# Value projections of a dilated attention: activation columns taken in token order, the head groups' orders made when the values are read back

## The chip, the cores and the metric

The kernel runs on one core of a Trainium2 chip. The metric is the device time of one execution in microseconds; the kernel before has a median of 1347.46 us over three runs (1345.95 to 1347.58). Engines are named as the profile names them: PE is TensorE (PEld its weight loads), DVE is VectorE, ACT is ScalarE, POOL is GpSimd, SP is SyncE, which here issues nearly all DMAs. A matmul on PE has two operands from on-chip memory (SBUF): a stationary one of 128 x 128, which a weight load puts into the array, and a moving one, which is streamed past it.

## The reference

One decoder block on x of 1024 tokens x 1024 features, batch 1. After a norm with a scale and shift from a conditioning vector, one projection `h @ w_in` gives q, k, v, a gate z, beta and a decay for eight heads of a gated delta rule (branch A), q, k, v and z for twelve heads of 64 features of a dilated sliding-window attention (branch B), and two merge gates. The two branches are projected, gated, added, projected once more and added to x; a final norm ends it. What matters here is branch B:

```python
DIL_CONFIGS = ((128, 1), (512, 4), (2048, 16))   # (window, dilation) of the head groups 0, 1, 2
...
qb, kb, vb, zb = ...                             # columns of h @ w_in
for gi, (win, dil) in enumerate(DIL_CONFIGS):    # four heads each
    o_g, lse_g = dilated_window_attention(qb[:, :, hs], kb[:, :, hs], vb[:, :, hs], win, dil)
```

Query t attends the keys t - j * dilation. So the tokens of a group fall into classes of equal remainder, and the kernel works through a group's tokens class by class: group 0 in token order, group 1 in four classes (t mod 4) of 256 tokens, group 2 in eight classes (t mod 8) of 128 tokens, where a mask does the rest of the dilation of 16.

## The kernel before, in words

Everything is fp32. A projection with full precision is made of three products: activations and weights are each split into a high part (fp32r) and a low remainder, and hi x hi, hi x lo and lo x hi are accumulated. The transposed activations hT (features on the 128 partitions, 1024 tokens along the free axis) lie in SBUF as eight pairs (hi, lo) of 128 x 1024 tiles, one pair for each block kk of 128 features.

Most projections are feature-major: the weights are stationary, hT is moving, and a tile of 128 features x 1024 tokens takes 48 matmuls of 128 x 512. The value projections of the attention, which the program calls B0, B1 and B2 for the head groups 0, 1, 2, are token-major: hT is stationary (`cols(hi)` and `cols(lo)`), the split weights (tiles named wh) are moving, 256 columns wide (272 for B0, which has beta and the decay in it). Each has eight tiles of 128 tokens, taken in pairs i2 = 0..3; a pair goes through the eight feature blocks with two tiles x three products each, so that a stage has 4 x 8 x 6 = 192 matmuls. In the profile they are the rows `pj<-wh,big`, where big is hT.

The stationary operand of such a matmul is 128 columns of hT. `v_cols` says which: for B0 128 neighbouring tokens, for B1 every fourth token, for B2 every eighth. So the PSUM tiles come out in the group's order. ACT copies each pair into one of two tiles big of 128 x 1024 (four token tiles of 256 values side by side), and at the stage's end SP writes both to a DRAM buffer vbd of 128 x 2048, as they lie. Much later `attn_group` reads them back, as they lie, when it has room for them, and the attention's last products take 64 columns of them as stationary operands.

All streams of work (one for each head, each weight unit, each attention worker) are generators; a scheduler at build time (`Sched`) books each instruction on an estimated clock and picks by priority, so the order on each engine is fixed in the program. At run time each engine takes its instructions in that order and waits at semaphores. The projections are the stream of lowest priority and fill PE. Between their matmuls stand the small products of the delta rule's recurrence (`rec_stream`: rows `sb<-sq,TT`, `sb<-sq,big`), where each step needs a result of DVE or ACT. The program order of the projections is in four parts, one for each pair of heads (`ORDER`): B0 is the third tile of the first part and B1 its last, B2 is the last of the second part.

Weights come by DMA into one of two tiles wr, are split by ACT (hi) and DVE (lo) into a pair of the six tiles wh, and are freed after their last matmul. A value projection holds three weight units, all six tiles wh, through its four pairs; they become free in the last pair, after kk = 2, 5 and 7.

Times in the profile have one line for nearly all instructions, line 96 (the helper `Engine.call`), so that tiles and shapes tell them apart.

Of the kernel before, what the change touches and what calls it, by code (L numbers as in the profile page):

```python
# [7 lines left out]
F32 = mybir.dt.float32  # L8
# [5 lines left out]
DRAM = bass.MemoryType.DRAM  # L14

P = 128
T = 1024
# [33 lines left out]
class Slots:  # L51
    """Live-tile accounting for one tag, so that a tile is asked for only when one is free."""

# [6 lines left out]
    def get(self, dtype=F32, shape=None, add=None, owed=0):  # L60
        """add: a tile that promises so many later ones; owed: one (1) of those."""
        while len(self.free_at) <= (0 if add is None else self.debt + add):
            yield lambda: len(self.free_at) > (0 if add is None else self.debt + add)
        self.debt += (add or 0) - owed
        self.free_at.sort()
        t = self.free_at.pop(0)
        if t > self.s.now():
            yield t
        self.count += 1
        return self.pool.tile(shape or self.shape, dtype, tag=self.tag, name=f"{self.tag}{self.count}")  # L70
# [15 lines left out]
class Engine:  # L86
    """An engine of the core whose issued work is also booked on an estimated clock."""

# [14 lines left out]
class Sched:  # L103
    """Orders the instructions: every stream is a generator that yields where it waits."""

# [69 lines left out]
    def chain(self, e, n=1):  # L175
        """n operations on engine e each need the result of the one before."""
        self.clk[e] += 125 * n
        self.cur.done[e] += 125 * n
        self.cur.last = max(self.cur.last, self.cur.done[e])
# [73 lines left out]
def hybrid_block_kernel(ctx: ExitStack, tc: tile.TileContext, x, c, norm_w, ada_w, ada_b, w_tiles, w_vb0, w_vb1,  # L253
# [26 lines left out]

    # ---- constants and small parameters
    cst = const([P, 1056], "cst")
# [26 lines left out]
    xd_d = [dp.tile([64, T], F32, name=f"xd{i}") for i in range(4)]  # L309
    vb_d = [dp.tile([P, 2048], F32, name=f"vbd{g}") for g in range(3)]  # L310
    ya_d = [dp.tile([P, T], F32, name=f"yad{h}") for h in range(H)]
# [22 lines left out]

    # ---- start: x, statistics, transposes
    def load_start():
# [62 lines left out]
    def consts_start():  # L399
        dve.memset(pw[:, 0], -0.5)  # L400
        dve.memset(pw[:, 1], 0.5)
        for i in range(2):
            pool.memset(TT[i], 0.0)
            pool.memset(Xb[i], 0.0)
        dve.memset(one_row, 1.0)
        yield ev_row
        # silu(c) on every partition
        for hf in range(2):
            pb = yield from sb.get()
            pe.matmul(pb, one_row, scb[1][0:1, hf * 512:(hf + 1) * 512], start=True, stop=True)  # L410
            yield
            if hf == 0:
                scb[0] = yield from big.get()
            act.activation(scb[0][:, hf * 512:(hf + 1) * 512], pb, AF.Silu)
            sb.put()
        big.put()
        S.set(ev_mod)
# [90 lines left out]

    # ---- weights: load, split into two exact parts
    class W:  # L510
# [44 lines left out]

    # ---- products with both operands split
    def three(pt, whi, wlo, khi, klo, first, last):
# [5 lines left out]

    # ---- the kinds of output tiles
    KT, QT, VT, ZT = {}, {}, {}, {}
# [71 lines left out]

    # ---- projection program
    prog = []
# [61 lines left out]

    def v_cols(g, i):
        """Token positions of tile i in the order of group g, as columns of the transposed activations."""
        if g == 0:
            return lambda t: t[:, i * P:(i + 1) * P]
        if g == 1:
            r, ub = divmod(i, 2)
            return lambda t: t.rearrange("p (u r) -> p r u", r=4)[:, r, ub * P:(ub + 1) * P]
        return lambda t: t.rearrange("p (u r) -> p r u", r=8)[:, i, :]

    def v_evac(pt, g, i2, last):
        vt = VB[g]
        n = 272 if g == 0 else 256
        src = pt.rearrange("p (a b) -> p a b", a=2)
        dst = vt[i2 // 2].rearrange("p (a b) -> p a b", a=4)
        a0 = (i2 % 2) * 2
        act.activation(dst[:, a0:a0 + 2, :], src[:, :, 0:256], AF.Copy)
        if g == 0:
            dve.tensor_copy(ba[:, 2 * i2:2 * i2 + 2, :], src[:, :, 256:272])
        pj.put()  # L720
        if last:
            if g == 0:
                S.set(ev_ba)
            yield
            for q in range(2):
                sp.dma_start(vb_d[g][:, q * T:(q + 1) * T], vt[q])
            big.put(2)
            S.set(ev_vbd[g])
# [3 lines left out]
    def projections():  # L732
        # the first tiles go contraction-outermost, behind the preparation of h
        pts = []
        for q in range(FIRST):
            kind, idx, u = prog[q]
# [37 lines left out]
        for n, (kind, idx, u) in enumerate(prog):  # L774
# [3 lines left out]
            if kind == "vB":  # L778
                w = 272 if idx == 0 else 256
                VB[idx] = []  # L780
                for _ in range(2):
                    t = yield from big.get(add=0)
                    VB[idx].append(t)
                for i2 in range(4):
                    pt = yield from pj.get()
                    for kk in range(8):
                        uu = u[kk // 3]
                        if i2 == 0:
                            yield uu.ev
                        c0 = (kk % 3) * w  # L790
                        hi, lo = hT[kk]
                        for i in (2 * i2, 2 * i2 + 1):
                            cols = v_cols(idx, i)
                            o = pt[:, (i % 2) * 512:(i % 2) * 512 + w]
                            pe.matmul(o, cols(hi), uu.hi[:, c0:c0 + w], start=kk == 0, stop=False)
                            pe.matmul(o, cols(hi), uu.lo[:, c0:c0 + w], start=False, stop=False)
                            pe.matmul(o, cols(lo), uu.hi[:, c0:c0 + w], start=False, stop=kk == 7)
                        if i2 == 3 and kk in (2, 5, 7):
                            wh.put(2)
                        yield S.now()  # L800
                    S.add(v_evac(pt, idx, i2, i2 == 3), 10, f"vB{idx}{i2}")
                continue
# [10 lines left out]
            S.add(finish(kind, idx, pt), 10, f"{kind}{idx}")  # L813
        # merge phase
        yield from tail_products()

    # ---- gates of the delta rule, for all heads
    def stats_stream():
# [41 lines left out]

    # ---- delta rule, one head
    DT, KP, NT, AT, VR = {}, {}, {}, {}, {}
# [21 lines left out]
    def d_stream(h):  # L884
        """exp of the sum of g over the tokens after the row's, up to the column's."""
        yield [ev_g, ev_stats]
# [70 lines left out]
    def inv_stream(p):  # L957
# [5 lines left out]
        yield  # L963
        # the inverse grows in the lower triangles, the factors stay in the upper ones
        pool.memset(xv[:, 0:T:33], 1.0)
# [103 lines left out]
    def qsum_stream(h):  # L1069
        """Squares of q summed over its features, tokens on the partitions."""  # L1070
        yield ev_q[h]
# [18 lines left out]
    def turn(src, dst, bounce):  # L1090
        """Transposes every 128 x 128 block: 32 x 32 blocks on VectorE, which then change places through DRAM.

        Columns of dst: (quarter of a block's rows, block, row in the quarter)."""
        t = yield from big.get()
# [20 lines left out]
    def rec_stream(h):  # L1115
# [55 lines left out]
        big.put(5)  # L1171
        # norm over the head, gate, feature-major
        q8, m8 = qss[:, h], mo[:, h]
# [19 lines left out]

    # ---- dilated attention
    OG = {}
# [3 lines left out]
    def attn_unit(g, i2, ti):  # L1199
        """Two tiles of 128 queries, feature tile ti (two heads, in the two halves of the rows)."""  # L1200
        qt, kt = QB[2 * g + ti], KB[2 * g + ti]
# [62 lines left out]
        if pend[g] == 8:  # L1264
            S.set(ev_og[g])

    def attn_group(g):
        yield [ev_vbd[g], ev_qb[2 * g]]
        VB[g] = []
        for q in range(2):  # L1270
            t = yield from big.get(owed=1)
            sp.dma_start(t, vb_d[g][:, q * T:(q + 1) * T])
            VB[g].append(t)
# [108 lines left out]

    # ---- merge and output
    YA, YB, MG, WO, M = {}, {}, {}, {}, {}
# [87 lines left out]
    def rows_stream():  # L1472
        """gate and the final norm's weights, along the free axis on every partition."""
        yield ev_mg[0]
# [53 lines left out]
    def tail_products():  # L1528
# [15 lines left out]

        # two tiles side by side while their operand is still being prepared
        for j, kk in [(j, k_ - 2 * j) for k_ in range(10) for j in range(2) if 0 <= k_ - 2 * j < 8]:
# [109 lines left out]
def _layout(inp):  # L1656
    """The arrays as the program takes them: moved around, never computed on."""
    import numpy as np
# [60 lines left out]
```

## Time and profile before

| | |
|---|---|
| median of three runs | 1347.46 us |
| span of the profiled execution, first to last instruction | 1343.9 us |
| own total of the profiled execution | not recorded apart; the median is 3.6 us above the span |
| PE busy | 1307.5 us, 97% of the span |
| PEld busy | 1095.1 us, 81% |
| DVE, ACT, POOL busy | 690.3, 494.3, 146.4 us |
| granted PE clock, mean | 0.995 |
| DMA | 137.65 MB, 102 GB/s on average |
| stage B0 | 76.4 to 100.9 us |
| stage B1 | 231.0 to 289.1 us, the recurrence of heads 0 and 1 beside it |
| stage B2 | 440.2 to 491.7 us, the end of the recurrence of heads 2 and 3 beside its first part |
| values read back | from 839.2, 872.8 and 941.7 us |

[...] A row of the timeline is a run of like instructions: start in us, length in us, engine, line, operation, tiles, count. Rows with DMA_DIRECT2D on SPq are the issues of DMAs, not the transfers.

### The profile page before, as it was taken

Reading aid. Unit: us, or ns where it says so; the run is one execution under the profiler, and the core shown is the slowest. Engines: PE = TensorE matmul, PEld = TensorE weight load, DVE = VectorE, ACT = ScalarE, POOL = GpSimd, SP = SyncE. Lnnn points to the kernel's source line nnn. Section 1 sums busy time; section 2 is a strip of 40 time slices with the busy share of each in tenths; the row PEclk is TensorE's granted clock in tenths of the full one; section 3 lists DMA queues with packets and bytes.
Section 4 is the critical chain, followed back from the end, with each engine's and each line's share of the span. In section 5 each row is a group of like instructions: output and inputs, shape, how many; then the busy total and the mean of one; then the engine's idle time right before and its main releaser. Section 6 shows DMA issues by size and latency. Waiting matters only on the chain.

```text
span 1343.9 us, 18856 instructions
## 1 busy us (share of the span) xinstructions
PE 1307.5 (97%) x7386; PEld 1095.1 (81%) x7386; DVE 690.3 (51%) x1437; ACT 494.3 (37%) x1054; POOL 146.4 (11%) x97
## 2 busy tenths in 40 slices
PE   5899899999999999999999999999999999999997
PEld 3698688998888998888888888877777888888886
DVE  6767762147873137873478734232323136745533
ACT  5637213246233226233462334253536432212211
POOL 4502100023000112000230002000000000001500
PEclk9899999999999999999999999999999999999999
DMA  9336421043321152322243212411111165342422
GB/s 361 105 120 180 103 87 47 25 136 120 105 77 35 32 188 67 106 72 71 86 138 106 78 49 94 144 62 33 64 38 35 41 222 159 119 141 107 152 99 94
DMA packets 72266, 137.65 MB, mean 102 GB/s; under 512 B 30161, under 2 KB 38769, under 8 KB 72178
## 3 DMA queue, kind: packets, MB, share of 16 engines
q1 hardware_dynamic: 72034, 136.20, 32.0%
q8 instruction: 58, 0.95, 0.3%
q14 instruction: 30, 0.25, 0.1%
q10 hardware_dynamic: 144, 0.26, 0.1%
HBM read 105.84 MB, written 30.59 MB: 102 GB/s over the span
## 4 chain that ended last, share of the span: by engine, by line
PE 90%; DMA 4%; DVE 4%; issue 1%; ACT 0%; SPq 0%; POOL 0%; POOLq 0%; DVEq 0%; ACTq 0%
PE pj L96 76%; PE sb L96 14%; DVE big L96 3%; DMA wr<-in_w_tiles_dram 1%; DMA vtd<-big 1%; DMA big<-in_ada_w_dram 1%; DVE wh L96 1%; DMA big<-in_x_dram 0%; DMA big<-grow 0%; SPq L96 0%; DVE mod L96 0%; DMA big<-vtd 0%; ACT wh L96 0%; ACT big L96 0%; POOL big L96 0%
## 5 line engine op out<-in xcount | busy, mean ns | idle before, releaser
L96 PE MATMUL pj<-big,wh 128*128 128x512 f32 x3840 | 941.9, 398 | 11.1 <-POOL big L96 6.3
L96 PEld LDWEIGHTS pj<-big,wh 128*128 128x128 f32 x3840 | 706.3, 189 | 157.4 <-POOL big L96 7.8
L96 ACT ACTIVATE wh<-wr 128x1024 fp32r<-128x1024 f32 (+3 forms) x96 | 95.6, 996 | 322.0 <-PE pj L96 301.6
L96 DVE TENSOR_TENSOR wh<-wr,wh 128x1024 fp32r<-128x1024 f32 (+3 forms) x93 | 114.8, 1236 | 158.2 <-ACT wh L96 158.0
L96 PE MATMUL pj<-wh,big 128*128 128x256 f32 (+2 forms) x702 | 155.7, 373 | 0.0
L96 PEld LDWEIGHTS pj<-wh,big 128*128 128x128 f32 x702 | 142.2, 267 | 5.3 <-POOL wh L96 0.4
L96 ACT ACTIVATE big<-big 128x1024 f32<-128x1024 f32 (+1 forms) x61 | 64.5, 1059 | 149.3 <-DVE big L96 117.9
L96 DVE SCALAR_TENSOR_TENSOR big<-pj,cw,big 128x1023 f32<-128x1023 f32 (+2 forms) x66 | 84.4, 1279 | 1.8 <-ACT big L96 0.3
L96 PEld LDWEIGHTS sb<-sq,big 128*128 128x128 f32 x464 | 63.0, 192 | 4.4
L96 PE MATMUL sb<-sq,big 128*128 128x128 f32 x464 | 65.5, 274 | 0.0
L96 DVE TENSOR_TENSOR big<-big,big 128x1024 f32<-128x1024 f32 (+3 forms) x40 | 55.0, 1381 | 15.4 <-ACT big L96 13.3
L96 ACT ACTIVATE big<-pj 128x1024 f32<-128x1024 f32 (+1 forms) x56 | 51.7, 923 | 29.3 <-PE pj L96 29.2
L96 ACT ACTIVATE mid<-sb 128x384 f32<-128x384 f32 (+5 forms) x75 | 34.1, 461 | 66.9 <-PE sb L96 66.5
L96 DVE SCALAR_TENSOR_TENSOR sq<-sq,gsm,sb 128x128 f32<-128x128 f32 x48 | 16.6, 345 | 81.8 <-PE sb L96 80.4
L96 POOL TENSOR_TENSOR wh<-wr,wh 128x1024 fp32r<-128x1024 f32 x3 | 9.0, 3009 | 398.2 <-ACT wh L96 398.1
L96 ACT ACTIVATE mid<-mid,sta 128x128 f32<-128x128 f32 (+1 forms) x96 | 42.2, 441 | 25.5 <-DVE sta L96 25.5
L96 DVE COPY big<-sb 128x256 f32<-128x256 f32 (+1 forms) x32 | 12.4, 389 | 74.0 <-PE sb L96 73.9
L96 PE MATMUL pj<-big,big 128*128 128x512 f32 x210 | 49.1, 389 | 0.0
L96 POOL TENSOR_TENSOR mo<-mo,pw 128x8 f32<-128x8 f32 x8 | 13.1, 1636 | 325.2 <-DVE mo L96 325.2
L96 PE MATMUL sb<-big,big 128*128 128x128 f32 (+4 forms) x365 | 45.5, 316 | 1.8 <-DVE big L96 1.8
L96 ACT ACT_TABLE_LOAD x29 | 37.2, 1283 | 26.2 <-DVE big L96 22.4
L96 PEld LDWEIGHTS pj<-big,big 128*128 128x128 f32 x210 | 39.4, 188 | 8.2
(124 smaller groups left out, 1115.1 us busy)
## 6 DMA issues: line engine op xcount, KB each, us to landing
wr<-in_w_tiles_dram SPq DMA_DIRECT2D x64, 512.0 KB, 3.8
big<-in_ada_w_dram SPq DMA_DIRECT2D x24, 512.0 KB, 9.0
big<-in_x_dram SPq DMA_DIRECT2D x16, 512.0 KB, 4.7
gd<-big SPq DMA_DIRECT2D x16, 512.0 KB, 5.0
big<-gd SPq DMA_DIRECT2D x16, 512.0 KB, 4.7
big<-grow SPq DMA_DIRECT2D x8, 512.0 KB, 5.1
vtd<-big SPq DMA_DIRECT2D x8, 512.0 KB, 3.0
big<-vtd SPq DMA_DIRECT2D x32, 128.0 KB, 3.7
```

The source lines that it names most:

```text
L96: r = f(*a, **k)
```

## The change

The three value projections take 128 neighbouring tokens as the stationary operand, in all groups. The DRAM buffers vbd become 1024 tokens x 256 values: row t holds token t. The write at a stage's end puts each token tile into its rows; the read makes the group's order by its access pattern (`v_load`).

```diff
-    vb_d = [dp.tile([P, 2048], F32, name=f"vbd{g}") for g in range(3)]
+    vb_d = [dp.tile([T, 256], F32, name=f"vbd{g}") for g in range(3)]
...
-    def v_cols(g, i):
-        if g == 0:
-            return lambda t: t[:, i * P:(i + 1) * P]
-        if g == 1:
-            r, ub = divmod(i, 2)
-            return lambda t: t.rearrange("p (u r) -> p r u", r=4)[:, r, ub * P:(ub + 1) * P]
-        return lambda t: t.rearrange("p (u r) -> p r u", r=8)[:, i, :]
...
     def v_evac(pt, g, i2, last):
...
+            rows = vb_d[g].rearrange("(i p) f -> p i f", p=P)
             for q in range(2):
-                sp.dma_start(vb_d[g][:, q * T:(q + 1) * T], vt[q])
+                sp.dma_start(rows[:, 4 * q:4 * q + 4], vt[q].rearrange("p (a f) -> p a f", a=4))
...
     def projections():
...
                         for i in (2 * i2, 2 * i2 + 1):
-                            cols = v_cols(idx, i)
+                            cs = slice(i * P, (i + 1) * P)
                             o = pt[:, (i % 2) * 512:(i % 2) * 512 + w]
-                            pe.matmul(o, cols(hi), uu.hi[:, c0:c0 + w], start=kk == 0, stop=False)
-                            pe.matmul(o, cols(hi), uu.lo[:, c0:c0 + w], start=False, stop=False)
-                            pe.matmul(o, cols(lo), uu.hi[:, c0:c0 + w], start=False, stop=kk == 7)
+                            pe.matmul(o, hi[:, cs], uu.hi[:, c0:c0 + w], start=kk == 0, stop=False)
+                            pe.matmul(o, hi[:, cs], uu.lo[:, c0:c0 + w], start=False, stop=False)
+                            pe.matmul(o, lo[:, cs], uu.hi[:, c0:c0 + w], start=False, stop=kk == 7)
...
+    def v_load(g, q, t):
+        t4 = t.rearrange("p (a f) -> p a f", a=4)
+        if g == 0:
+            sp.dma_start(t4, vb_d[g].rearrange("(i p) f -> p i f", p=P)[:, 4 * q:4 * q + 4])
+        elif g == 1:
+            src = vb_d[g].rearrange("(b p r) f -> r p b f", b=2, r=4)
+            for a in range(2):
+                sp.dma_start(t4[:, 2 * a:2 * a + 2], src[2 * q + a])
+        else:
+            sp.dma_start(t4, vb_d[g].rearrange("(p r) f -> p r f", r=8)[:, 4 * q:4 * q + 4])
...
     def attn_group(g):
...
-            sp.dma_start(t, vb_d[g][:, q * T:(q + 1) * T])
+            v_load(g, q, t)
```

The order of the instructions on PE, DVE, ACT and POOL is the same in both kernels, one for one. Only SP's queue differs. At the end of B1, where the values of group 1 (vbd_119) are written (two tiles big, between the loads of the next weights wr), the two issues stay where they were:

```order
 L96 DMA wr_2429<-in_w_tiles_dram 128x1024
-L96 DMA vbd_119<-big_2001 128x1024
-L96 DMA vbd_119<-big_2002 128x1024
+L96 DMA vbd_119<-big_2001 128x4x256
+L96 DMA vbd_119<-big_2002 128x4x256
 L96 DMA wr_2470<-in_w_tiles_dram 128x1024
```

Each partition's 1024 values now go to four places of 256 values (1 KB) in place of one of 4 KB. At the place where the values of group 1 are read back for the attention, two issues became four, again between the same loads of weights:

```order
 L96 DMA wr_7173<-in_w_tiles_dram 128x1024
-L96 DMA big_7338<-vbd_119 128x1024
-L96 DMA big_7340<-vbd_119 128x1024
-L96 DMA wr_7344<-in_w_tiles_dram 128x1024
-L96 DMA wr_7561<-in_w_tiles_dram 128x1024
+L96 DMA big_7338<-vbd_119 128x2x256 x2
+L96 DMA big_7341<-vbd_119 128x2x256 x2
+L96 DMA wr_7346<-in_w_tiles_dram 128x1024
+L96 DMA wr_7563<-in_w_tiles_dram 128x1024
```

Groups 0 and 2 are read with two issues each as before, group 0 in pieces of 1 KB, group 2 in runs of 4 KB (four rows that are neighbours).

## The prediction

> **What bounds the kernel now.** I read the page first: the engines' busy times and the chain that ended last.
>
> ```profile
> PE 1307.5 (97%) x7386; PEld 1095.1 (81%) x7386; DVE 690.3 (51%) x1437; ACT 494.3 (37%) x1054; POOL 146.4 (11%) x97
> PE 90%; DMA 4%; DVE 4%; issue 1%; ACT 0%; SPq 0%; POOL 0%; POOLq 0%; DVEq 0%; ACTq 0%
> ```
>
> PE is busy nearly throughout and makes 90% of the chain that ended last. What PE saves in a stage is saved in the end, unless another engine was just hidden behind that stage. Next, PE's matmuls grouped by shape, for the value projections (`pj<-wh,big`; the row of 272 columns is B0, that of 256 columns is B1 and B2 together):
>
> ```profile
> L96 PE MATMUL pj<-wh,big 128*128 128x256 f32 x384 | 100.7, 409 | 0.0
> L96 PE MATMUL pj<-wh,big 128*128 128x272 f32 x192 | 24.5, 288 | 0.0
> ```
>
> Twice as many matmuls of fewer columns take four times as long: 100.7 / 384 = 262 ns of busy time each against 24.5 / 192 = 128 ns. The two rows differ in width, and in the step between the stationary columns. So I look at the weight loads, first by stage for these tiles alone (columns: stretch, its length, PE busy, PEld busy, DVE, ACT, POOL, clock, DMA share, GB/s), then by duration in B0, B1 and the last part of B2:
>
> ```profile
> 76.40:100.90 24.50, 24.39 (x194) 24.13 (x193) 1.95 (x2) 2.62 (x3) 0.00 (x0) 1.00 0.39 131
> 230.96:289.11 58.15, 51.31 (x193) 47.18 (x194) 3.13 (x3) 2.74 (x3) 0.00 (x0) 1.00 0.12 38
> 440.16:491.73 51.57, 49.10 (x193) 47.24 (x193) 3.13 (x3) 2.12 (x2) 0.00 (x0) 1.00 0.23 72
> ```
>
> ```profile
> L96 PEld LDWEIGHTS pj<-wh,big 128*128 128x128 f32 x105 | 13.2, 188 | 0.0
> L96 PEld LDWEIGHTS pj<-wh,big 128*128 128x128 f32 x192 | 47.2, 329 | 0.0
> L96 PEld LDWEIGHTS pj<-wh,big 128*128 128x128 f32 x90 | 21.7, 337 | 0.0
> ```
>
> A load of 128 neighbouring columns lasts 188 ns (B0), of every fourth 329 ns (B1), of every eighth 337 ns (B2). The clock is 1.00 in all three stages, so it isn't the clock. In B1 and B2 the loads are back to back (47.2 us for 192, 246 ns each) and the matmuls wait for them. Steps of 4 and of 8 cost the same.
>
> What would 256 columns cost with a dense load? The timeline of the kernel's end has such matmuls, and that of B2's undisturbed part the slow ones:
>
> ```profile
> 470.04 21.85 PE L96 MATMUL pj<-wh,big 128*128 128x256 f32 x90
> 491.73 22.41 PE L96 MATMUL pj<-big,wh 128*128 128x512 f32 x98
> 513.98 0.60 PE L96 MATMUL sb<-cst,big 128*128 128x128 f32 x4
> ```
>
> ```profile
> 1331.59 1.96 PE L96 MATMUL sb<-big,big 128*128 128x256 f32 x15
> 1333.39 1.24 PE L96 MATMUL sb<-wh,big 128*128 128x256 f32 x9
> ```
>
> Start to start, 15 dense ones take 1333.39 - 1331.59 = 1.80 us, 120 ns each; 90 strided ones take 491.73 - 470.04 = 21.69 us, 241 ns each. B0's 272 columns at 24.13 / 192 = 126 ns agree with 120 for 256.
>
> **The change part by part.** *The loads become dense.* B1 and B2 need 47.18 + 47.24 = 94.4 us of PE for 384 pairs of load and matmul; at 120 ns they need 46.1. Gross gain 48.3 us.
>
> *The changes between streams.* A dense run pays something where PE goes over to the recurrence's products, which a strided run partly hides. In the second pair's recurrence, beside dense matmuls of 512 columns:
>
> ```profile
> 417.85 0.70 PE L96 MATMUL pj<-big,wh 128*128 128x512 f32 x2
> 418.39 0.61 PE L96 MATMUL sb<-sq,big 128*128 128x128 f32 x4
> ```
>
> In the long run after B2 one such matmul takes (513.98 - 491.73) / 98 = 227 ns; two between small products take 418.39 - 417.85 = 0.54 us, 0.09 more than 2 x 0.227. B1 has 25 such runs and B2 has 12 (rows of the timeline from 230.96 on, the last of them the one at 470.04), so 37 x 0.09 = 3.3 us come back.
>
> *The recurrence beside it.* A step of heads 0 and 1 in B1, PE's rows and then ACT's (in brackets the idle time ahead and what ended it):
>
> ```profile
> 245.97 0.60 PE L96 MATMUL sb<-sq,TT 128*128 128x128 f32 x4
> 246.33 1.67 PE L96 MATMUL pj<-wh,big 128*128 128x256 f32 x6
> 247.83 1.05 PE L96 MATMUL sb<-sq,big 128*128 128x128 f32 x8
> ```
>
> ```profile
> 246.56 0.59 ACT L96 ACTIVATE big<-pj 128x512 f32<-128x512 f32 x1
> 247.04 0.28 ACT L96 ACTIVATE sq<-sb 128x128 f32<-128x128 f32 x1
> ```
>
> PE goes from the four TT products to the eight that need ACT's two copies `sq<-sb` in 1.86 us: 0.36 for its own four and 1.50 for six strided matmuls. With dense ones it is there after 0.36 + 6 x 0.12 + 0.09 = 1.17 us. The second copy ends 247.32 - 245.97 = 1.35 us after the start, since a copy of the value projection (0.59) stands ahead of it in ACT's queue; so half of the eight wait some 0.2 us, and this happens only where a pair of value tiles is copied out. The other hand-overs lack that copy, which leaves 1.35 - 0.59 = 0.76 us against 1.17. And the row at 417.85 shows a cover of 0.54 us between two dependent groups, where the dense B1 has 0.81. I take 1 us for all waits. The bounds are 0 and 0.3 us at each of the 37 runs, 11.1 us; behind a waiting product stand only the next value matmuls, on PE itself. Nearest to the rows is the low end.
>
> *The next weights.* All six tiles wh are held until the last pair, so the split of the next weights sits in the last 30 matmuls:
>
> ```profile
> 98.36 1.23 DVE L96 TENSOR_TENSOR wh<-wr,wh 128x1024 fp32r<-128x1024 f32 x1 [1.07 <-ACT wh L96]
> ...
> 484.49 1.06 ACT L96 ACTIVATE wh<-wr 128x1024 fp32r<-128x1024 f32 x1 [3.48 <-PE pj L96]
> 485.58 1.23 DVE L96 TENSOR_TENSOR wh<-wr,wh 128x1024 fp32r<-128x1024 f32 x1 [8.51 <-ACT wh L96]
> ```
>
> In B2 the split ends at 486.81 and PE needs it at 491.73: 4.92 us of room, of which 30 x 0.121 = 3.6 go. 1.3 us are left, as many as B0, dense already, has between 98.36 + 1.23 = 99.59 and its end at 100.9, without a stall (24.39 us of its 24.50 are busy with these tiles). B1 has more (the recurrence is between). Behind that wait in ACT's and DVE's queues are only the recurrence's last steps. Cost 0; if the cover were gone, one split, 1.06 + 1.23 = 2.3 us in each stage.
>
> *Where the room goes.* All instructions in B1 and in B2, columns as above:
>
> ```profile
> 230.96:289.11 58.15, 58.15 (x310) 58.15 (x309) 13.46 (x41) 17.30 (x56) 0.97 (x1) 1.00 0.12 38
> 440.16:491.73 51.57, 51.57 (x242) 51.57 (x240) 11.17 (x28) 10.25 (x30) 7.07 (x4) 1.00 0.23 72
> ```
>
> DVE has 13.5 of 58.2 us in B1 and 11.2 of 51.6 in B2, ACT 17.3 and 10.3, so neither carries a backlog out of the stage when it is 22 us shorter. What runs on DMA time across B2's end is the row of g for the next head:
>
> ```profile
> 487.28 0.38 SPq L96 DMA_DIRECT2D big<-grow  x1
> ...
> 494.65 1.68 DVE L96 TENSOR_TENSOR_SCAN big<-big,cst 128x128 f32<-128x128 f32 x5
> ```
>
> It is issued 4.4 us before the stage's end, later 0.9 before it, lands (5.1 us, below) about 4.2 after the end, and its scan on DVE begins 2.9 after now: about 1.3 us late. Behind it in DVE's queue are convolutions and splits of tiles that PE needs from 10 us after the end on. Cost 0; without that cover 1.3 us.
>
> *The DMAs.* The six writes and the reads of groups 0 and 1 go in pieces of 1 KB, and six issues of reads become eight. The DMAs by tile (count, KB each, us from issue to landing), and the first read beside the first products that use it:
>
> ```profile
> big<-grow SPq DMA_DIRECT2D x8, 512.0 KB, 5.1
> ...
> big<-vtd SPq DMA_DIRECT2D x32, 128.0 KB, 3.7
> ...
> vbd<-big SPq DMA_DIRECT2D x6, 512.0 KB, 5.3
> ```
>
> ```profile
> 839.21 1.27 SPq L96 DMA_DIRECT2D big<-vbd  x2
> ...
> 880.79 0.88 PE L96 MATMUL sb<-mid,big 128*64 128x128 f32 x12
> ```
>
> The reads of vtd have pieces of 1 KB: 3.7 us for 128 KB. So a transfer of 512 KB lies between 5.3 us (no change) and 4 x 3.7 = 14.8 (four of these one after the other), nearer the lower, since a fourth of the bytes takes 3.7 as well. The read at 839 has 41 us until its use, so even 2 x 14.8 us is hidden. Each more issue costs SP 1.27 / 2 = 0.6 us, ahead of a weight load that two tiles wr cover. Below nothing the cost can't be, as nothing gets shorter there. Cost 0 to 2 us (a write ahead of the weight loads); I take 0.
>
> *Sum.* 48.3 - 3.3 - 1 = 44.0 us. The span goes from 1343.9 to 1299.9. The median of the runs is 3.6 above that span, so **1303.5 us**.
>
> [...]
>
> **The rivals.** *The waits take over*: the hand-overs of the recurrence set the pace in B1 and B2, each near its bound. Gain 48.3 - 3.3 - 11.1 = 33.9, and with late splits 2 x 2.3 less: 29.3 to 33.9, about 1316 us. For it: PE's cover of each hand-over nearly halves. Against: the 0.54 us of cover at 417.85 without a stall, and B0's end.
>
> *Half the gain*, in one of two ways. Only the step of 8 pays, so that B1 keeps its time: 47.24 - 23.04 - 12 x 0.09 = 23.1 us less, 1324 us; against it B1's 329 ns. Or the 188 ns of a dense load aren't hidden: 384 x (0.246 - 0.188) = 22.3 us less, 1325 us; against it B0. [...]
>
> *The change doesn't do what it says*: the 256-column matmuls are slow for a reason other than the step, and nothing moves, 1347 us. Against it: the 120 ns at the kernel's end.
>
> *Slower*: the pieces of 1 KB block the DMA queues ahead of weight loads, at the three writes and the reads of groups 0 and 1. If they went one after the other at the row of vtd, 1 MB would take 8 x 3.7 = 29.6 us; the cover is the tile that PE is on, 48 x 0.227 = 10.9 us; so PE would stall 18.7 us at each of five places, 93.5 us, and the time would be 1303.5 + 93.5 = 1397 us. It decides the sign from 44 / 5 = 8.8 us at each place on, that is when 1 MB takes 19.7 us or more. Against: it takes about twice 5.3 now, and the DMA engines are 0.12 and 0.23 busy in B1 and B2.
>
> **How the numbers follow.** Forecast 0.85, the waits take over 0.08, half the gain 0.03, nothing moves 0.02, slower 0.02. The range holds the forecast with its unknowns. Low end: no price for the changes between streams and no waits, gain 48.3, and 1 us for the spread of the runs: 1298. High end: the waits' upper bound without late splits, gain 33.9: 1313. A difference over 0.2%, 2.7 us, is about what a measurement of this kernel can tell from no change: faster 0.96 (the first three cases), same 0.02, slower 0.02.
>
> **What would show it.** In the changed profile: LDWEIGHTS of `pj<-wh,big` at about 188 ns in all three stages; the row of 256 columns at about 46 us busy in place of 100.7 (some more, as runs beside small products overlap); B1 about 36 us long, B2 about 28; DVE, ACT and POOL with the same busy times; the stretch from 492 to the end as long as before. Wrong would be it if the loads stay at 330 ns, or if B1 stays above 45 us with PE waiting for DVE or ACT at `sb` rows, or if a later stretch grows by more than 2 us, first of all where `big<-vbd` or `vbd<-big` is followed by a late `wr`.

## The result, and the profile after

The changed kernel takes 1300.57 us in the median of four runs (1299.39 to 1300.83), the kernel before 1347.05 (1345.95 to 1347.58, four runs). The ratio is 0.9654, with a 95% interval of 0.964 to 0.9667: 46.5 us or 3.5% faster. The profiled execution has a span of 1299.0 us and a time of 1300.81.

The page of the changed kernel, engines' busy times and the chain that ended last:

```profile
PE 1261.6 (97%) x7386; PEld 1049.0 (81%) x7386; DVE 690.9 (53%) x1437; ACT 494.3 (38%) x1054; POOL 145.4 (11%) x97
PE 82%; issue 7%; DVE 6%; DMA 3%; POOL 1%; ACT 1%; SPq 0%; POOLq 0%; DVEq 0%; ACTq 0%
```

PE lost 45.9 us of busy time and PEld 46.1; DVE, ACT and POOL kept theirs within 1 us. PE is still busy for 97% of the span and stays the bound. The chain has less of PE in it than before (82% against 90%): at a wait of PE that is shown below it goes over to the other engines, back to POOL at 267 us, and the 71.6 us for which POOL had then been idle are counted as issue. The groups by shape of the changed kernel, B1 and B2 first, then B0, then all weight loads of these tiles (126 for matmuls of 512 columns among them), and those of the kernel before:

```profile
L96 PE MATMUL pj<-wh,big 128*128 128x256 f32 x384 | 54.8, 290 | 0.0
...
L96 PE MATMUL pj<-wh,big 128*128 128x272 f32 x192 | 24.5, 288 | 0.0
...
L96 PEld LDWEIGHTS pj<-wh,big 128*128 128x128 f32 x702 | 95.9, 189 | 5.2 <-DVE big L96 0.2
```

```profile
L96 PEld LDWEIGHTS pj<-wh,big 128*128 128x128 f32 x702 | 142.2, 267 | 5.3 <-POOL wh L96 0.4
```

The row of 256 columns fell from 100.7 to 54.8 us; that of B0, which the change leaves alone on PE, is the same to the tenth. A load's mean fell from 267 to 189 ns. Neighbouring matmuls overlap in these rows: 384 of 290 ns make 111 us, and the group is busy for 54.8; so busy times and distances from start to start are compared here, not mean durations. The stages by windows, first of the changed kernel (ahead of B1 nothing differs; columns: stretch, length, PE, PEld, DVE, ACT, POOL busy, clock, DMA share, GB/s), then of the kernel before:

```profile
231.21:266.84 35.63, 35.63 (x310) 35.63 (x308) 12.97 (x39) 16.83 (x55) 0.00 (x0) 1.00 0.17 50
266.84:418.86 152.02, 151.24 (x957) 126.99 (x955) 103.03 (x215) 60.32 (x130) 20.92 (x12) 1.00 0.34 100
418.86:447.02 28.16, 28.16 (x242) 28.16 (x240) 9.51 (x26) 10.15 (x30) 7.07 (x4) 1.00 0.28 93
447.02:1299.00 851.98, 844.51 (x4697) 691.94 (x4695) 417.01 (x866) 306.04 (x667) 67.21 (x41) 1.00 0.31 99
```

```profile
289.11:440.16 151.05, 151.05 (x955) 127.07 (x955) 102.02 (x212) 60.13 (x129) 19.95 (x12) 1.00 0.33 98
491.73:1343.90 852.17, 844.59 (x4696) 692.00 (x4695) 415.17 (x864) 305.76 (x667) 68.09 (x41) 1.00 0.31 98
```

| stretch | before, us | after, us | difference |
|---|---|---|---|
| start to B1 | 230.96 | 231.21 | +0.25 |
| B1 | 58.15 | 35.63 | -22.52 |
| between B1 and B2 | 151.05 | 152.02 | +0.97 |
| B2 | 51.57 | 28.16 | -23.41 |
| B2 to the end | 852.17 | 851.98 | -0.19 |
| span | 1343.9 | 1299.0 | -44.9 |

All of the gain is in the two stages, and 0.97 us of it is given back between them. Of these, 0.78 us are one wait of PE behind B1; the other 0.19 us are busy time (151.24 us against 151.05) that no row explains. The timeline of PE has the wait:

```profile
270.43 18.42 PE L96 MATMUL pj<-big,wh 128*128 128x512 f32 x80
289.62 0.66 PE L96 MATMUL sb<-cst,big 128*128 128x128 f32 x4 [0.78 <-ACT big L96]
```

PE waits 0.78 us for a result of ACT (in brackets the idle time and what ended it), ahead of the transposes of a new head's k. Before, it went from its 80 matmuls to these transposes without a wait.

### The profile page after: what moved, and what is told of

It is laid out like the page before. It is cut to its first block, busy times and chain, and to the rows that moved or that the text cites. A ratio compares the mean times of both kernels' runs of the same rounds, so it can differ in the third digit from the quotient of the medians.

```text
span 1299.0 us, 18858 instructions
## 1 busy us (share of the span) xinstructions
PE 1261.6 (97%) x7386; PEld 1049.0 (81%) x7386; DVE 690.9 (53%) x1437; ACT 494.3 (38%) x1054; POOL 145.4 (11%) x97
## 4 chain that ended last, share of the span: by engine, by line
PE 82%; issue 7%; DVE 6%; DMA 3%; POOL 1%; ACT 1%; SPq 0%; POOLq 0%; DVEq 0%; ACTq 0%
PE pj L96 69%; PE sb L96 13%; DVE big L96 4%; DMA big<-in_x_dram 1%; DMA vtd<-big 1%; DVE wh L96 1%; POOL big L96 1%; DVE mod L96 1%; DMA big<-grow 0%; ACT big L96 0%; DVE mid L96 0%; DMA big<-otd 0%; SPq L96 0%; POOL mo L96 0%; DMA otd<-big 0%
## 5 line engine op out<-in xcount | busy, mean ns | idle before, releaser
L96 PE MATMUL pj<-wh,big 128*128 128x256 f32 (+2 forms) x702 | 109.5, 307 | 0.0
L96 PEld LDWEIGHTS pj<-wh,big 128*128 128x128 f32 x702 | 95.9, 189 | 5.2 <-DVE big L96 0.2
L96 DVE TENSOR_TENSOR mid<-big 64x31 f32<-64x31 f32 (+15 forms) x124 | 41.1, 332 | 9.0 <-POOL big L96 5.6
```

The lines of the kernel that those rows point to most:

```text
L96: r = f(*a, **k)
```

## The experiments

Each is told against runs of the kernel before on the same chip, beside it (medians 1346.2 to 1346.5 us; a single run beside the two wide kernels).

### Each stage alone

```diff
# b1_dense, against the changed kernel (B2 strided again, B1 dense)
+    def v_cols(g, i):
+        if g < 2:
+            return lambda t: t[:, i * P:(i + 1) * P]
+        return lambda t: t.rearrange("p (u r) -> p r u", r=8)[:, i, :]
...
+                if g == 2:
+                    sp.dma_start(vb_d[g].rearrange("(p r) f -> p r f", r=8)[:, 4 * q:4 * q + 4], v4)
```

> B1 takes neighbouring tokens, B2 still every eighth; the buffers hold token rows and the reads make the order, as in the change. Theory (the cost sits in the loads of stationary columns at a step, on PE alone, and adds up by stage): B1 shrinks by 22.5 us as in the changed kernel, B2 stays at 51.6, and the stall of 1 us after B1 comes with it: 1347.0 - 22.5 + 1.0 = 1325.5 us, between 1324 and 1327. [...] Rival (part of the gain came from the transfers): outside 1324 to 1327, and the two halves don't add up to 46.5.

> B2 takes neighbouring tokens, B1 still every fourth. Theory: B2 shrinks by 23.4 us, nothing after it stalls: 1347.0 - 23.4 = 1323.6 us, between 1322 and 1325. Rival (only the step of 8 paid): 1300.6, the whole gain. Rival (the transfers have a part in it): the gains of the two halves differ from 46.5 us in sum by more than 2.

b2_dense is the mirror image: B1 strided, its values written class by class with four DMAs, B2 dense. Measured: b1_dense 1324.67 us (ratio 0.9836, 0.9822 to 0.9849), b2_dense 1323.02 us (0.9823, 0.9809 to 0.9836), beside 1346.52. The gains are 21.9 and 23.5 us, 45.4 in sum; the whole change gave 46.5. So each stage pays for itself, and a step of 4 costs about as much as a step of 8. The rival of the prediction by which only the step of 8 pays is out.

### The transfers alone, and the loads alone

```diff
# dma_only, against the changed kernel: v_cols as in the kernel before, and in v_evac
+                if g == 1:
+                    src = vb_d[g].rearrange("(b p r) f -> r p b f", b=2, r=4)
+                    for a in range(2):
+                        sp.dma_start(src[2 * q + a], v4[:, 2 * a:2 * a + 2])
+                elif g == 2:
+                    sp.dma_start(vb_d[g].rearrange("(p r) f -> p r f", r=8)[:, 4 * q:4 * q + 4], v4)
# dense_old_dma, against the kernel before
-        if g == 0:
-            return lambda t: t[:, i * P:(i + 1) * P]
...
+        return lambda t: t[:, i * P:(i + 1) * P]
```

> Both stages still take their tokens at a step; the values go to the token rows of the new buffers (group 1 by four writes) and are read back by the new patterns. Theory (the pieces of 1 KB are hidden): 1347.0 within 1 us. Rival (the pieces cost, and the change's gain is net of them): 1349 or more, with a late weight load behind vbd rows.

> The columns are neighbours in all three stages, the buffers and transfers are those of the kernel before. Left out: the order of the values of groups 1 and 2 is not made, so the attention of these groups reads other tokens' values; the work is the same. Theory: the change's time, 1300.6 within 1 us. Rival (the new transfers cost): 1 to 3 us below the change. Rival (they help by shorter transfers): above it.

dma_only: 1346.56 us beside 1346.52, ratio 0.9997 (0.9988 to 1.0006). dense_old_dma: 1301.43 us, 0.9662 (0.9649 to 0.9675), which can't be told from the change's 0.9654. The reads of dma_only are those of the change, its writes are not (group 1 in four writes, group 2 in runs of 4 KB); the change's own writes are tested by dense_old_dma, which lacks them and lies 0.9 us from the change. The transfers neither cost nor gain anything that these runs resolve. The DMAs of the changed kernel by tile (count, KB each, us from issue to landing), and SP's issues where group 1 is read back:

```profile
vbd<-big SPq DMA_DIRECT2D x6, 512.0 KB, 5.4
...
big<-vbd SPq DMA_DIRECT2D x4, 512.0 KB, 5.6
...
big<-vbd SPq DMA_DIRECT2D x4, 256.0 KB, 5.2
```

```profile
828.14 1.97 SPq L96 DMA_DIRECT2D big<-vbd  x4
846.12 25.05 SPq L96 DMA_DIRECT2D wr<-in_w_tiles_dram  x2
```

Pieces of 1 KB land in the time of pieces of 4 KB (5.4 us against 5.3 for the writes), and the four issues end 16 us ahead of SP's next weights.

### Which step costs what

Steps of 2 and of 3 fp32 lie between the dense load (120 ns a pair) and the steps of 4 and 8 (246 ns a load in both stages). My forecasts, 1300 to 1304 us for step2 and 1324 for step3, rest on an assumption about the load that no run shows.

```diff
# step2: B1 and B2 take every second token of a block of 256
+        return lambda t: t.rearrange("p (b u r) -> p b r u", b=4, r=2)[:, i // 2, i % 2, :]
# step3: every third
+        return lambda t: t[:, 80 * i:80 * i + 382:3]
```

> As the change, but B1 and B2 take every second token (two classes in each block of 256 tokens), 8 bytes from column to column; the writes put them into token rows. [...] Rival (any step takes the slow way, 241 ns): 1346.5. Rival (the cost grows evenly with the step, half way between 1 and 4 at 2): around 1315.

> As the change, but B1 and B2 take every third token, 12 bytes apart, from a start of 80 columns times the tile's number. Left out: the values of groups 1 and 2 are those of other tokens; the work is the same. [...] Rival (any step but 1, or any step over 2): 1346.

step2 takes 1302.26 us (0.9668, 0.9652 to 0.9683), step3 1322.49 (one run). B2's run without other products between, of the changed kernel (step 1), of step2 and of step3:

```profile
436.14 11.04 PE L96 MATMUL pj<-wh,big 128*128 128x256 f32 x90
447.02 22.41 PE L96 MATMUL pj<-big,wh 128*128 128x512 f32 x98
```

```profile
437.86 11.05 PE L96 MATMUL pj<-wh,big 128*128 128x256 f32 x90
448.75 21.49 PE L96 MATMUL pj<-big,wh 128*128 128x512 f32 x94
```

```profile
452.40 15.93 PE L96 MATMUL pj<-wh,big 128*128 128x256 f32 x90
468.17 22.42 PE L96 MATMUL pj<-big,wh 128*128 128x512 f32 x98
```

| step of the columns, fp32 | 1 | 2 | 3 | 8 (kernel before) |
|---|---|---|---|---|
| start to start, us for 90 | 10.88 | 10.89 | 15.77 | 21.69 |
| ns a pair of load and matmul | 121 | 121 | 175 | 241 |

A step of 4 costs as much as one of 8 (47.18 and 47.24 us for 192 loads in the kernel before). Up to there the pair's time goes nearly with the step: 175 / 3 = 58 and 241 / 4 = 60 ns for each fp32 of step. By these two numbers I estimate 117 to 121 ns for a load at a step of 2, no more than the dense pair's 121, so that beside 256 columns it would not show; measured, the pair takes 121. The loads' own durations in these runs of 90, of the changed kernel, step2 and step3, go the same way (337 ns at a step of 8):

```profile
L96 PEld LDWEIGHTS pj<-wh,big 128*128 128x128 f32 x90 | 10.9, 192 | 0.0
```

```profile
L96 PEld LDWEIGHTS pj<-wh,big 128*128 128x128 f32 x90 | 10.9, 195 | 0.0
```

```profile
L96 PEld LDWEIGHTS pj<-wh,big 128*128 128x128 f32 x90 | 15.8, 262 | 0.0
```

If any step were slow, step2 would lie at 1346, and if steps below 4 cost nothing, step3 would lie at 1301; both are out: a step of 2 costs nothing beside 256 columns, 3 costs 54 ns a pair, and 4 costs as much as 8. Why the cost grows up to a step of 4 and is the same at 8 was not shown; pairs of neighbours at a far step would say more, and weren't tried.

### Whether the load hides behind a wider matmul

```diff
# wide_dense, against the changed kernel; wide_step, the same against dma_only
-                        c0 = (kk % 3) * w
+                        c0, w = ((kk % 3) * 272, 272) if idx == 0 else (0, 512)
```

> As the change, but the matmuls of B1 and B2 are 512 columns wide: the moving operand is the first 512 columns of each weight tile. Left out: the values of groups 1 and 2 are not the projection's. Theory: each pair of load and matmul takes 227 ns in place of 120, 384 x 0.107 = 41 us more than the change: 1342 us, within 4.

> The same width of 512 with the strided columns of the kernel before (every fourth, every eighth). Left out as in wide_dense. Theory (a load runs beside the matmul of the pair before, the longer of the two sets the pace): 241 to 248 ns against 227, 384 x 0.014 to 0.021 = 5 to 8 us over wide_dense, about 1348. Rival (the strided load's extra 121 ns add to the matmul): 46 us over wide_dense, 1388.

1342.9 and 1352.21 us, one run each. The undisturbed end of B2, of wide_dense and of wide_step:

```profile
469.89 19.34 PE L96 MATMUL pj<-wh,big 128*128 128x512 f32 x84
489.06 21.02 PE L96 MATMUL pj<-big,wh 128*128 128x512 f32 x92
```

```profile
477.33 21.08 PE L96 MATMUL pj<-wh,big 128*128 128x512 f32 x84
498.25 21.06 PE L96 MATMUL pj<-big,wh 128*128 128x512 f32 x92
```

A pair takes 19.17 / 84 = 228 ns dense and 20.92 / 84 = 249 ns strided. So the same strided load costs 120 ns beside 256 columns and 21 ns beside 512: load and matmul run side by side, and the longer one sets the pace, plus a little (the load's 241 ns against the matmul's 228, and 249 for the pair). 384 x 21 ns are 8.1 us; the two single runs differ by 9.3, where 5 to 8 were expected.

### A step in the moving operand

```diff
# moving_step, against the changed kernel: q and k of groups 1 and 2
+                mv = m[:, sl] if r == 1 else m.rearrange("p (u r) -> p r u", r=r)[:, hf * r // 2:(hf + 1) * r // 2, :]
...
-        act.activation(dst, perm(pt, g), AF.Copy, scale=scale)
+        act.activation(store[i], pt, AF.Copy, scale=scale)
```

> As the change, but the q and k projections of groups 1 and 2 (8 tiles of 48 matmuls of 512) take the moving operand, the activations, in the groups' order (steps of 4 and 8) instead of ordering on the copy out of PSUM. Theory that a step costs any read of the array alike: 512 columns at 1.88 ns are 0.96 us in place of 0.227, 384 x 0.74 = 283 us more, 1584. Rival (only the load of the stationary operand is slow): 1300.6 within 3 us.

1386.16 us (one run), 85.6 above the change: both theories missed. Eighteen matmuls of 512 columns at a step of 4 in moving_step, and the same eighteen in the changed kernel:

```profile
833.79 8.55 PE L96 MATMUL pj<-big,wh 128*128 128x512 f32 x18
842.16 0.51 PE L96 MATMUL sb<-cst,mid 128*128 128x128 f32 x3
```

```profile
829.53 4.38 PE L96 MATMUL pj<-big,wh 128*128 128x512 f32 x18
833.75 0.49 PE L96 MATMUL sb<-cst,mid 128*128 128x128 f32 x3
```

8.37 / 18 = 465 ns against 4.22 / 18 = 234. The matmul with its moving operand at a step of 4 takes twice the time, 0.91 ns a column against 0.46; a load at a step of 8 takes 241 / 128 = 1.88 ns a column, and one at a step of 4 about as much (47.18 us for 192 loads of 128, 1.92 ns). The price of a column at a far step is not one number for both operands, and why stays open.

### The microsecond given back after B1

```diff
# late_split, against the changed kernel: the third weights after B1 are split during the next tile
             yield u.raw_ev
+            if n_ + FIRST == late[0]:
+                yield late[1]
```

> The change with one edit in the order: the split of the weights of the third tile after B1, which stood at B1's end, is put off by the better part of a tile. Theory (the stall of 0.78 us at 289.6 in the changed kernel comes from DVE, whose split of these weights beside POOL's product takes 2.64 us and pushes the convolution behind it): the stall goes and the time is 1299.6 to 1300.6, too little for a verdict; the trace shows it. Rival (the stall comes from elsewhere, from POOL's norm or from ACT's tables): it stays at 0.7 us or more.

1300.69 us in the median of five (0.9673, 0.9655 to 0.9691), no difference that can be told from the change; three of the five lie at 1300.0 to 1300.7 and two at 1304.6 and 1305.2, which stays unexplained. The wait itself comes with the short B1: PE's idle time ahead of all transposes of this form (`sb<-cst,big`) that ACT's results ended is 1.3 us in the changed kernel and 1.2 to 1.3 in other kernels with the same short B1 (b1_dense, step2, moving_step), and 0.5 us in the kernel before and in those with a longer B1 (b2_dense, dma_only, step3, wide_dense, wide_step). Rows of DVE, ACT and POOL, of the changed kernel, with B1's end at 266.84, and of the kernel before, with it at 289.11:

```profile
267.48 0.37 ACT L96 ACTIVATE big<-sb,gsm 128x128 f32<-128x128 f32 x1 [1.12 <-DVE sq L96]
267.74 0.59 ACT L96 ACTIVATE big<-pj 128x512 f32<-128x512 f32 x1
...
268.98 1.90 POOL L96 TENSOR_TENSOR big<-big,mo 128x1024 f32<-128x1024 f32 x1
...
269.31 2.64 DVE L96 TENSOR_TENSOR wh<-wr,wh 128x1024 fp32r<-128x1024 f32 x1 [1.87 <-ACT wh L96]
...
271.88 0.28 DVE L96 TENSOR_TENSOR big<-sb,big 128x128 f32<-128x128 f32 x1
...
279.89 1.25 DVE L96 STREAM_TRANSPOSE big<-big 128x1024 f32<-128x1024 f32 x1 [3.73 <-POOL big L96]
281.06 2.25 DVE L96 TENSOR_TENSOR wh<-wr,wh 128x1024 fp32r<-128x1024 f32 x1
283.23 3.91 DVE L96 SCALAR_TENSOR_TENSOR big<-pj,cw,big 128x1023 f32<-128x1023 f32 x3
```

```profile
289.31 0.60 ACT L96 ACTIVATE big<-pj 128x512 f32<-128x512 f32 x1 [0.59 <-PE pj L96]
...
289.85 1.90 POOL L96 TENSOR_TENSOR big<-big,mo 128x1024 f32<-128x1024 f32 x1
...
290.88 1.95 DVE L96 TENSOR_TENSOR wh<-wr,wh 128x1024 fp32r<-128x1024 f32 x1 [2.57 <-ACT wh L96]
...
293.01 0.29 DVE L96 TENSOR_TENSOR big<-sb,big 128x128 f32<-128x128 f32 x1 [0.18 <-PE sb L96]
...
304.37 3.91 DVE L96 SCALAR_TENSOR_TENSOR big<-pj,cw,big 128x1023 f32<-128x1023 f32 x3
```

The split of the third weights starts 2.47 us after B1 in place of 1.77. It waits for ACT, whose copy of the last value tiles (`big<-pj`), ahead of the split in its queue, starts 0.90 us after B1 in place of 0.20: before, this copy waited for PE's last matmul, now it stands behind a copy of the recurrence, which waits for DVE.

The split also lasts 2.64 us in place of 1.95. In both kernels it starts while POOL's product (`big<-big,mo`) runs, and lies beside it for 1.57 us in place of 0.87; a split with no POOL product beside it takes 1.22 us, so it is longer by 1.42 and 0.73, nearly the whole overlap. The changed kernel has seven splits of 128 x 1024 that start while POOL has a product of that size running, and each is longer by the overlap less 0.13 to 0.15 us. Two splits start before POOL's product, and there the split is no longer than alone and the product is: at 132.28 us by 0.83 for 0.97 us beside a split of 1.18 (2.73 us against 1.90), and in the rows below (2.41 us where it comes first) by 0.41 for 0.55 us beside a split of 1.22:

```profile
642.08 1.22 DVE L96 TENSOR_TENSOR wh<-wr,wh 128x1024 fp32r<-128x1024 f32 x1
642.75 2.82 POOL L96 TENSOR_TENSOR big<-big,cst 128x1024 f32<-128x1024 f32 x1 [14.81 <-ACT big L96]
```

So in these rows the one that comes second hardly gets on until the first is done.

With both delays DVE's last step of the recurrence comes 5.04 us after B1 in place of 3.90. All that hangs on it (the norm on POOL, the transposes on DVE, which wait for POOL, and behind them the convolution of k) keeps these 1.1 us, and the convolution starts 16.39 us after B1 in place of 15.26. The transposes on PE wait for it. In late_split:

```profile
270.02 0.29 DVE L96 TENSOR_TENSOR big<-sb,big 128x128 f32<-128x128 f32 x1 [2.81 <-PE sb L96]
...
276.82 2.55 POOL L96 TENSOR_TENSOR mo<-mo,pw 128x8 f32<-128x8 f32 x1
...
281.87 1.25 DVE L96 STREAM_TRANSPOSE big<-big 128x1024 f32<-128x1024 f32 x1 [1.79 <-POOL big L96]
283.04 3.87 DVE L96 SCALAR_TENSOR_TENSOR big<-pj,cw,big 128x1023 f32<-128x1023 f32 x3
...
289.40 0.65 PE L96 MATMUL sb<-cst,big 128*128 128x128 f32 x4 [0.34 <-ACT big L96]
```

With the split out of the way the recurrence's last step came 1.6 us earlier after B1's end (266.61 here). But the edit moved POOL's order too: its norm started later and took 2.55 us, and the convolution began where it had begun. PE's transposes begin 22.79 us after B1's end as in the changed kernel (22.78), and its wait went to 0.34 only because the new order puts two more matmuls between the two (8 + 4 + 84 in place of 8 + 6 + 80, 0.45 us). Neither expectation is met as it stands: the wait did not go, and it did not stay at 0.7. So the first link (the split) is shown; that it is the only one is not, and DVE's wait for POOL is the nearer one.

## Why the prediction was right

The forecast was 1303.5 us in a range of 1298 to 1313; measured 1300.57. By its steps:

- **The loads become dense**, 384 pairs at 120 ns: the run of 90 gives 121 ns. Right, and the mechanism is shown from both sides: with the strided loads alone put back nothing is gained (dma_only), with the dense loads alone nearly everything is (dense_old_dma), and the cost comes and goes with the step (step2, step3).
- **The changes between streams**, 0.09 us at 37 places, 3.3 us: over-sized a little. Six matmuls between two small products, in the changed kernel:

```profile
239.94 0.60 PE L96 MATMUL sb<-sq,TT 128*128 128x128 f32 x4
240.30 0.96 PE L96 MATMUL pj<-wh,big 128*128 128x256 f32 x6
241.09 1.06 PE L96 MATMUL sb<-sq,big 128*128 128x128 f32 x8
```

  241.09 - 240.30 = 0.79 us, 0.07 over 6 x 0.12. The two stages gained 45.9 us together, where the loads alone give 48.3, so the 37 places took 2.4 us.
- **The recurrence's waits**, 1 us: none is seen, PE is busy for all of both stages (35.63 and 28.16 us). The step above is the one that the prediction looked at, and takes 1.15 us from four to eight products where 1.17 was forecast for PE alone.
- **The next weights**, cost 0: right at B2, where the split ends at 445.82, 1.2 us ahead of the stage's end (1.3 forecast). In B1 it ends at 263.66, 3.2 us ahead.
- **Where the room goes**, cost 0: this step failed, by the wait of 0.78 us behind B1. I asked whether DVE carries a backlog out of the stage by its busy share (13.5 of 58.2 us), and not what each of its instructions at the stage's end has queued behind it. One split of 2.64 us after B1 delays a chain of DVE and POOL that PE meets 22.8 us later. The late scan after B2, forecast at 1.3 us, came 2.7 us later after the stage's end than before (452.64 - 447.02 against 494.65 - 491.73) and cost PE nothing.
- **The DMAs**, cost 0 to 2 us, taken as 0: right, dma_only 1346.56 against 1346.52.
- **From span to time**: I put 3.6 us on the span, the median less the profile's span. The profiled executions since have 1.8 to 1.9 us between them (1300.81 and 1299.0, 1347.68 and 1345.8 in dma_only), so the profiled execution before was, by inference, near 1345.7, one of the fastest. This, 1.8 us, then 0.2 us between the profiled execution and the median, and 0.9 us of the sum (44.9 saved by the spans, 44.0 forecast) are the 2.9 us between 1303.5 and 1300.57.
- **Luck**: the sum is nearer than its terms. The 1 us taken for waits inside the stages did not come, and 0.97 us that the sum had at nothing came between them; that the two cancel is chance.

Of the rivals, the waits came to nothing inside the stages, and to 0.78 us behind B1, in place of 11. Half the gain is out by b1_dense, and in its other form by the dense pairs of B1 and B2 at 121 ns, less than the 188 ns of a load; wide_step shows the same from the other side (a load that isn't hidden would have cost 120 ns more beside 512 columns too). Nothing moves and slower are out by the result and by dma_only.

## What to carry to other kernels

Where a weight load's duration differs between two groups of the same shape, look at the step of its columns in memory before anything else: here the load at a step of 4 or 8 fp32 set the pace at 241 to 246 ns a pair against 121, and the reordering that it did cost nothing when a DMA that was there anyway took it over. How much a far step costs depends on the matmul beside it (120 ns a pair at 256 columns, 21 at 512), so narrow matmuls are where to look; a step of 2 cost nothing here (121 ns a pair as at 1). After a stage gets shorter, go through the queue of each engine at its end instruction by instruction: a low busy share did not show the one split that came too late and then met POOL's product.

## What the runs showed of the hardware that I had not expected

- The cost of a load grows with the step in between: 121 ns a pair at 2 as at 1, 175 at 3, 241 at 8 (the loads themselves 195, 262 and 337 ns, 192 at 1).
- A strided moving operand isn't free either: 465 ns against 234 for 512 columns at a step of 4, twice the time and not the 0.96 us that the load's price would have given.
- Transfers in pieces of 1 KB landed as fast as in pieces of 4 KB: 5.4 us against 5.3 for 512 KB written.
- In the rows of this kernel a split on DVE and a product of 128 x 1024 on POOL hardly run side by side: the one that starts second is longer by nearly the whole overlap, DVE's split 2.64 us against 1.22 alone, the product 2.82 against 2.41. POOL's norm took 2.55 us beside a split in late_split against 1.64 alone. These are rows of the traces; no run was made to test it.
